# Relative-bias lines in 16 DRAM copies in place of 128, each bias tile read by eight transfers of 16 partitions

## The chip, the cores and the metric

The kernel runs on one core of a Trainium2 chip. The metric is the device time of one execution in microseconds (us); several executions are timed and the median is taken. TensorE (PE) does the matrix products, VectorE (DVE), ScalarE (ACT) and GpSimd (POOL) the elementwise work; DMA transfers are issued from the queues of SyncE (SP), POOL and ACT and carried out by 16 DMA engines.

## What is computed

Two transformer blocks over 256 tokens with 1024 features, in float32. Block 1 has a differential attention and a stick-breaking attention, each followed by a mixture of many small experts (PEER). Block 2 has four layers; their mixers are dsa (16 heads, one shared key/value head, keys chosen by an index score), swa (a window of 128 keys with sinks), mla (latent attention), and dsa again, each followed by a feed-forward part. The change touches the relative bias, which dsa and swa add to their logits:

```python
def t5_bucket(rel):
    n = jnp.maximum(rel, 0)
    ...
    return jnp.where(n < max_exact, n, large)

# dsa
    rel = pos[None, :, None] - sel
    bias = jnp.moveaxis(rel_bias[t5_bucket(rel)], -1, 1)
    logits = jnp.einsum('bqhd,bqjd->bhqj', qb, kg).astype(jnp.float32) * scale + bias
    logits = jnp.where((rel >= 0)[:, None], logits, -jnp.inf)
# swa
    rel = qi - kj
    in_band = (rel >= 0) & (rel < WINDOW)
    bias = jnp.transpose(rel_bias[t5_bucket(rel)], (2, 0, 1)).reshape(B_KV_HEADS, group, WINDOW, 2 * WINDOW)
```

The bias depends on query and key by their distance alone. So one line of 383 values for each of the 16 heads holds it all, and the row of query p is the line shifted by p.

## The kernel before

**Products and weights.** Each float32 product is made of three products of float32r parts: a weight chunk (512 KB, [128, 1024]) is loaded as raw, cast to whi (mostly on ACT, L133) and the rest taken as wlo = raw - whi (DVE or POOL, L135). The class Stream (L83) does this in the order of use: the loads go to SP's queue (L105) into three raw buffers, so a chunk's load starts when the cast and the split of the chunk three places ahead have read their buffer. TensorE multiplies the parts in `mm` (L228). The projections that make feature-major tiles (ps_fm) and those that accumulate outputs (acc) both take their chunks from this stream: in_a_wo is the output projection of the differential attention, in_peer_q the query projection of the PEER behind it.

**Order.** The program is written head by head, and a scheduler sets the order in which each engine has its instructions; an engine then works strictly in that order. The scheduler has its own simulated times of transfers, and so a change of the transfers alone can move other instructions.

**The bias lines.** `bias_lines` (L1020) runs once, in `diff_attention` at step s == 5 of ten (L644). It makes the 16 lines of 383 values by one small product, adds to them a line of masks for dsa and for swa (mk_dsa, mk_swa, 16 partitions of 383 values), and writes each to a DRAM tile (line_dsa, line_swa), one copy per query, 128 in all, 3064 KB each, from POOL's queue (L1034). In the ten steps run at once, for different heads: the projections and rotations (stage_p), the logits and the softmax (stage_l), and the weighted values (stage_t) that end in `out_parts`, which puts the head's output into oT (L481, on ACT). The output projection follows (`acc_wo`), with `x` normalised behind it.

**The reads.** `load_bias` (L1078) gives a tile B [128, 16, 256]: partition p gets, for each head, 256 values of copy p of the line, starting at 127 - p. As copy p lies 16*383 elements behind copy p - 1, one access pattern with a step of 16*383 - 1 per partition reads all of it in one transfer of 2048 KB (L1081) from POOL's queue. It is called at the start of `dsa` (L1103, layers 0 and 3) and of `swa` (L1225). Right behind it on POOL's queue come small constants: in dsa cmask (L1108, the causal mask, to which the index score is added, L1142), blk (L1109, a block matrix of ones for sums over 64 features), the gains gq and gk (L1111, L1112) and gmlp; in swa blk (L1229), gq and gk (L1231, L1232), the sinks and gmlp. B itself is needed later, head by head: in dsa POOL adds the masked score to it (mb, L1183 and L1186), in swa DVE adds it to the logits (L1306, L1309). Between the index score and these the dsa layer finds the best keys in eight rounds on DVE; ps_ks is the sum of the squared keys by blk, ps_pT the transposed weights of a head.

Of the kernel before, what the change touches and what calls it, by code (L numbers as in the profile page):

```python
# [10 lines left out]
F32 = mybir.dt.float32  # L11
# [8 lines left out]
P = 128  # L20
# [15 lines left out]
# which engine splits: GpSimd takes the lower parts of these chunks, VectorE the upper parts of those  # L36
# [46 lines left out]
class Stream:  # L83
    """Weight chunks in the order of their use: loaded ahead, split into two float32r parts ahead.

    A chunk's parts take a slot of the base pool, or of the pool that a phase lends (for its own chunks)."""
# [55 lines left out]
    def queue_behind(self, ins, n=4):  # L142
        """the next splits stand behind this instruction of the vector engine"""
        self.behind, self.n_behind = ins and ins.ins, n
# [5 lines left out]
    def lend(self, pool, bufs, names):  # L150
        """slots of a phase's pool, for the chunks from here on that bear its names"""
        self.pools.append([pool, bufs, []])
        c = self.pos
        while c < len(self.plan) and self.plan[c][0] in names:
            c += 1
        self.lent_until = c
# [5 lines left out]
    def get(self, *keys, ahead=2):  # L162
        """the parts of the next chunks, which keys name; all chunks before them are used up"""
        c = self.pos
        for k, key in enumerate(keys):
            assert self.plan[c + k] == key, (self.plan[c + k], key)
        for pool in self.pools:
            pool[2] = [d for d in pool[2] if d >= c]
        self._fill(c + len(keys) - 1 + ahead)
        assert self.split >= c + len(keys), (keys, self.split)  # L170
        self.pos += len(keys)
        return [self.done.pop(c + k) for k in range(len(keys))]
# [3 lines left out]
def tile_two_blocks(ctx: ExitStack, tc: tile.TileContext, t: dict, out: bass.AP, dbg=None):  # L176
# [40 lines left out]
    def log_exp_table(after=None):  # L217
        """the set that holds both Ln and Exp, from here on"""
# [17 lines left out]
    class Parts:  # L236
        """feature-major activations [1024, 256] in two float32r parts, by feature chunk d and token tile"""
# [16 lines left out]
    def to_hT(src, tt, hT, make=None):  # L254
        """src [128 tokens, 1024] -> feature-major parts, columns of token tile tt; make(half) fills half of src"""
# [18 lines left out]
    def proj_fm(hT, *key, M=P):  # L274
        """feature-major projection of one chunk: PSUM [M, 256]"""
# [14 lines left out]
    def proj_fm_first(hT, keys, outs):  # L290
        """the first chunks of a phase, a token tile at a time, into outs, SBUF [M, 256] each"""
# [22 lines left out]
    def acc_rows(chunks, accs, first, ahead=2, chain=None, keep=4, stop=False):  # L314
        """accs[tt][half] [128 tokens, 512] += lhs^T (128 rows) @ chunk [128, 1024], for (key, lhs(tt, part)) in chunks

        With a chain, these are the last chunks: chain(tt) follows for each token tile, the first one's beside the
        products of the second, of which the last (keep steps) wait for its transposes to have been issued."""
# [3 lines left out]
        tail = 2 if chain else 0  # of these chunks the first half of the columns comes first  # L322
# [26 lines left out]
    def acc_wo(key, oT, chain, ahead=3):  # L349
        """the output projection, a token tile at a time; chain(tt, acc) follows"""  # L350
# [7 lines left out]
    def lend(px, bufs, *names):  # L358
        """more slots for the weights of this phase"""
# [12 lines left out]
    def add_residual(tt, acc, hf, alpha=None, scale=None):  # L372
        """a half of x: x * alpha + acc, or x + acc * scale"""
# [7 lines left out]
    def rsqrt_small(dst, src, eps, scale):  # L381
        """dst = 1 / sqrt(src * scale + eps)"""
# [3 lines left out]
    def norm_residual(tt, acc, gbc, bbc, sp):  # L386
        """x = layer norm of x * alpha + acc, up to its last step, which comes back: last(half)"""
# [16 lines left out]
    def rms_to_hT(tt, gbc, hT, sp):  # L404
# [4 lines left out]
        for hf in range(2):  # h takes the squares first  # L409
# [9 lines left out]
    def gained_to_hT(tt, gbc, hT, sp, spare):  # L419
        """x * gain -> hT; the square of the rms factor, which a squared relu lets through, comes back  # L420

        spare: two PSUM banks that nothing needs any more"""
# [16 lines left out]
    def bcast(pool, src, n, tag, queue=nc.gpsimd):  # L439
        """a [n] row of DRAM on all partitions"""  # L440
# [8 lines left out]
    # ---------------------------------------------------------------- attention pieces  # L449
    def transposes_pair(p_sb, sp):  # L450
        """p_sb [128 q, 2, 384] -> SBUF [128 k, 2, 384]: (k0,q0) (k0,q1) (k1,q1)"""
# [8 lines left out]
    def av(o, pTs, h, tt, v):  # L460
        """o [128 q, dv] = p @ v for one head and query tile"""
# [6 lines left out]
    def out_parts(o_sb, g, oT, gain=None):  # L468
        """o_sb [128 t, 2 (tile), 128 features] -> feature-major parts of group g"""
# [17 lines left out]
    def softmax_sums(L, sp, src=None):  # L487
        """L [128 q, 2, 128 + width] (tile 0 | tile 1): p unnormalised, of src or in place; sums [128, tile, 2]"""
# [13 lines left out]
    def softmax_pair(L, sp):  # L502
        """p unnormalised in place, reciprocals of the sums"""
# [5 lines left out]
    def logits_pair(q_of, k_of):  # L509
        """PSUM [128 q, 2 heads, 384]: tile 0 on keys 0..127, tile 1 on keys 0..255"""  # L510
# [7 lines left out]
    def pv_group(g, p_sb, ri, v, oT, sp):  # L518
        """p @ v of a pair of 64-wide heads, normalised, transposed into oT"""
# [13 lines left out]
    # ---------------------------------------------------------------- block 1, layer 0: differential attention  # L533
    def diff_attention(hT):
        with ExitStack() as px:
# [10 lines left out]
            # the constants come behind the first weights  # L546
# [53 lines left out]
            def stage_l(g):  # L600
                qr, kr = stt.pop(g)
                ps = logits_pair(lambda h: qr[h * 64 : h * 64 + 64, :], lambda h: kr[h * 64 : h * 64 + 64, :])
                # the first 64 queries of a tile do not see the last 64 keys of its range
# [53 lines left out]
    # ---------------------------------------------------------------- block 1, layer 1: stick-breaking attention  # L657
# [74 lines left out]
    # ---------------------------------------------------------------- PEER  # L732
    def peer(layer, hT, last):
        J1 = 72  # H of the columns from here on waits in DRAM while the gates take their place
# [4 lines left out]
        with ExitStack() as px:  # L739
# [120 lines left out]
            def gate():  # L860
                """G[:, j, t] = sum over the selections of token t of the gate at (i, j): into X, or times what X holds"""
# [134 lines left out]
            for b in range(NB - 1):  # L996
                nxt = split_s(b + 1)
                if b == NA - 1:
                    # what Xa held is used up: x comes back, and more slots for the weights
# [19 lines left out]
    # ---------------------------------------------------------------- block 2  # L1019
    def bias_lines():  # L1020
        """one line per head of the relative bias, in DRAM, a copy per query: entry m is for rel = 255 - m"""
        with tc.tile_pool(name="bl", bufs=1, side="right") as bl:
# [6 lines left out]
            for nm in ("dsa", "swa"):  # L1029
# [3 lines left out]
                ln = dpool.tile([P, 16, 383], F32, name=f"line_{nm}")  # L1033
                nc.gpsimd.dma_start(ln.rearrange("p h m -> h p m"), mk.unsqueeze(1).to_broadcast([16, P, 383]))  # L1034
# [6 lines left out]
    def rope_tables():  # L1041
        """cosines and sines of the latent attention's rope, and both times the gain of q's rope features"""
        with tc.tile_pool(name="bl", bufs=1, side="right") as bl:
# [5 lines left out]
            # angles: position * frequency, reduced to [-pi, pi]  # L1049
# [11 lines left out]
            # cos first: sin(ang + pi/2); the multiple of 2 pi is taken before the quarter turn is added  # L1061
# [16 lines left out]
    def load_bias(pool, line):  # L1078
        B = pool.tile([P, 16, S], F32, name="B")
        la = line[:, :, :]  # L1080
        nc.gpsimd.dma_start(B, bass.AP(la.tensor, la.offset + 127, [[16 * 383 - 1, P], [383, 16], [1, S]]))  # L1081
# [16 lines left out]
    def dsa(a, layer, hT):  # L1098
        with ExitStack() as px:
# [49 lines left out]
            # k: normalised over its 64 features, on both halves of the partitions  # L1149
# [201 lines left out]
    def mla(layer, hT):  # L1351
        with ExitStack() as px:
# [14 lines left out]
            # latents, token-major  # L1367
# [34 lines left out]
            def rope(dst, src, tt, nh):  # L1402
                """dst, src [128, nh, 32]: rotation of the halves of 16 by the token's angles"""
# [179 lines left out]
    # ---------------------------------------------------------------- the two blocks  # L1583
# [22 lines left out]
def _fm(w, cols):  # L1606
    """[1024, *] columns -> [128, 8 * len(cols)]: feature-major chunk"""
# [130 lines left out]
```

## Time and profile before

| | |
|---|---|
| median of 3 runs | 3167.72 us (3162.14 to 3167.91) |
| span of the profiled execution | 3171.6 us |
| TensorE busy | 3045.5 us (96%) |
| VectorE busy | 2083.6 us (66%) |
| ScalarE busy | 1666.1 us (53%) |
| GpSimd busy | 316.6 us (10%) |
| moved by DMA | 551 MB, 174 GB/s |

The profile is one execution, so its span is a few microseconds from the median. A busy share is a mean over stages with different limits: an engine at 53% of the whole can still be what others wait for in one stage. The rows on which the prediction rests are in a section of their own below. In them, a line of a timeline has the start, the duration, the engine, the line of the kernel, the operation, output and inputs, and in brackets how long the engine had been idle and for what it waited; a line of DMA issues has the size of one transfer and the time from issue to landing.

### The profile page before, as it was taken

The numbers are of one execution on the slowest core, as the hardware profiler recorded it, in microseconds if no ns is written. First come the engines' busy times: TensorE is split into PE (matmuls) and PEld (weight loads), VectorE is DVE, ScalarE is ACT, GpSimd is POOL, SyncE is SP. The second block draws the span as 40 slices with busy tenths as digits, with TensorE's granted clock in tenths as the row PEclk, the third lists the DMA queues.
The fourth block names the chain that finished last, engine by engine and source line by source line (L and its number), as shares of the span: only waits on it lengthen the run. The fifth ranks groups of instructions, "written<-read, shape, count | busy, mean of one in ns | idle before, by whom it ended". The sixth has DMA issues, their size and how long they took to land.

```text
span 3171.6 us, 51266 instructions
## 1 busy us (share of the span) xinstructions
PE 3045.5 (96%) x19968; PEld 2749.4 (87%) x19968; DVE 2083.6 (66%) x3603; ACT 1666.1 (53%) x2844; POOL 316.6 (10%) x246
## 2 busy tenths in 40 slices
PE   8699999999999899999999999999999979999999
PEld 7599999978887789999988887889889968998898
DVE  5379867775555769957766555755566565556654
ACT  5434568744443634558845444554545555554553
POOL 1400000010001310000010002400120021003200
PEclk9899999999999999999999999999999999999999
DMA  6855554476655435554476654445526532654364
GB/s 202 134 161 184 174 183 165 167 264 205 225 187 179 141 125 176 177 183 167 166 252 218 231 189 155 151 160 186 184 76 216 188 108 81 194 187 148 121 201 137
DMA packets 157636, 551.05 MB, mean 174 GB/s; under 512 B 18880, under 2 KB 19712, under 8 KB 157392
## 3 DMA queue, kind: packets, MB, share of 16 engines
q1 hardware_dynamic: 135216, 489.42, 46.3%
q0 software_dynamic: 12112, 41.54, 5.4%
q10 hardware_dynamic: 10064, 16.81, 1.5%
q8 instruction: 157, 2.57, 0.3%
q14 instruction: 87, 0.71, 0.1%
HBM read 523.59 MB, written 24.10 MB: 173 GB/s over the span
## 4 chain that ended last, share of the span: by engine, by line
PE 79%; DMA 9%; DVE 6%; ACT 3%; issue 2%; POOL 1%; SPq 0%; DVEq 0%; ACTq 0%; POOLq 0%
PE acc L228 31%; PE ps_h L228 23%; PE ps_fm L228 16%; PE ps_g L228 4%; DMA hb<-h_dram 3%; ACT whi L133 1%; DVE wlo L135 1%; PE ps_av L228 1%; POOL wlo L135 1%; PE ps_l L228 1%; DMA raw<-in_a_wo_dram 1%; DMA raw<-in_dsa_in_dram 1%; DMA raw<-in_b_kq_dram 1%; DMA raw<-in_peer_q_dram 1%; PE ps_xT L262 1%
## 5 line engine op out<-in xcount | busy, mean ns | idle before, releaser
L133 ACT CAST whi<-raw 128x1024 fp32r<-128x1024 f32 (+1 forms) x908 | 947.9, 1046 | 1014.3 <-PE acc L228 273.3
L135 DVE TENSOR_TENSOR wlo<-raw,whi 128x1024 fp32r<-128x1024 f32 (+1 forms) x854 | 1043.3, 1225 | 622.7 <-ACT whi L133 621.1
L228 PE MATMUL ps_h<-hT,whi 128*128 128x256 f32 x4096 | 751.5, 284 | 0.0
L228 PE MATMUL ps_fm<-hT,whi 128*128 128x256 f32 x3424 | 664.6, 286 | 17.3 <-ACT kq L686 5.4
L228 PEld LDWEIGHTS ps_h<-hT,whi 128*128 128x128 f32 x4096 | 639.1, 191 | 1.0
L228 PEld LDWEIGHTS ps_fm<-hT,whi 128*128 128x128 f32 x3424 | 559.3, 192 | 36.6 <-DVE hT L234 6.0
L228 PE MATMUL ps_h<-hT,wlo 128*128 128x256 f32 x2048 | 584.0, 285 | 0.0
L228 PE MATMUL acc<-whi,S_parts 128*128 128x512 f32 x1984 | 537.7, 392 | 0.0
L228 PE MATMUL ps_fm<-hT,wlo 128*128 128x256 f32 (+1 forms) x1936 | 533.0, 285 | 0.0
L228 PEld LDWEIGHTS acc<-whi,S_parts 128*128 128x128 f32 x1984 | 372.8, 188 | 83.8
L228 PEld LDWEIGHTS ps_h<-hT,wlo 128*128 128x128 f32 x2048 | 391.8, 191 | 0.2
L228 PEld LDWEIGHTS ps_fm<-hT,wlo 128*128 128x128 f32 (+1 forms) x1936 | 369.7, 191 | 1.4 <-issue 0.5
L228 PE MATMUL acc<-wlo,S_parts 128*128 128x512 f32 x992 | 309.5, 393 | 5.6 <-DVE wlo L135 5.5
L135 POOL TENSOR_TENSOR wlo<-raw,whi 128x1024 fp32r<-128x1024 f32 (+1 forms) x78 | 196.1, 2525 | 1057.2 <-ACT whi L133 986.3
L228 PEld LDWEIGHTS acc<-wlo,S_parts 128*128 128x128 f32 x992 | 185.9, 188 | 49.1 <-DVE wlo L135 7.8
L228 PE MATMUL acc<-whi,hh 128*128 128x512 f32 x512 | 162.6, 393 | 0.0
L228 PE MATMUL acc<-whi,hl 128*128 128x512 f32 x512 | 161.1, 392 | 0.6 <-DVE hl L234 0.6
L228 PE MATMUL acc<-wlo,hh 128*128 128x512 f32 x512 | 161.3, 391 | 0.0
L891 DVE TENSOR_SCALAR AB<-iota,selT 128x128 f32<-128x128 f32 x512 | 142.0, 343 | 17.2 <-PE ps_g L228 17.1
L895 ACT ACTIVATE AB<-iota,selT 128x128 f32<-128x128 f32 x384 | 122.9, 392 | 36.6 <-PE ps_g L228 35.9
L228 PE MATMUL acc<-whi,oT 128*128 128x512 f32 x384 | 129.0, 420 | 12.4 <-ACT oT L481 9.7
L228 PE MATMUL ps_g<-AB 128*128 128x128 f32 x1024 | 133.8, 275 | 0.0
(353 smaller groups left out, 3207.8 us busy)
## 6 DMA issues: line engine op xcount, KB each, us to landing
raw<-in_peer_u_dram SPq DMA_DIRECT2D x256, 512.0 KB, 3.6
raw<-in_peer_v_dram SPq DMA_DIRECT2D x256, 512.0 KB, 4.3
raw<-in_up_dram SPq DMA_DIRECT2D x128, 512.0 KB, 4.2
raw<-in_dn_dram SPq DMA_DIRECT2D x128, 512.0 KB, 4.3
raw<-in_dsa_in_dram SPq DMA_DIRECT2D x30, 512.0 KB, 4.0
h_dram<-hs ACTq DMA_DIRECT2D x56, 256.0 KB, 2.2
hb<-h_dram POOLq DMA_DIRECT2D x56, 256.0 KB, 4.0
raw<-in_a_qk_dram SPq DMA_DIRECT2D x16, 512.0 KB, 3.7
```

Of the source, the lines that this page charges most:

```text
L133: self.last_hi = self.nc.scalar.copy(hi[:, :n], t[:, :n])
L135: lo_eng.tensor_tensor(lo[:, :n], t[:, :n], hi[:, :n].bitcast(F32), ALU.subtract)
L228: pe["last"] = nc.tensor.matmul(o, lhsT, rhs, start=start, stop=stop)
L262: pe["tr"] = nc.tensor.transpose(ps[:, c * P : (c + 1) * P], src[:, d * P : (d + 1) * P], ident)
L891: nc.vector.tensor_scalar(A[:, i], iota, selT[:, 0, tk : tk + 1], selT[:, 2, tk : tk + 1], ALU.is_equal, ALU.mult)
L895: nc.scalar.activation(B[:, i], iota, AF.Abs, bias=selT[:, 1, tk : tk + 1], scale=-1.0)
```

## The change

The DRAM tile of a line holds 16 copies in place of 128, and the write makes 16 (383 KB in place of 3064 KB). A transfer that steps through the copies can now serve 16 partitions. So B is read by eight transfers, each of 16 partitions and 256 KB, each starting q = 0, 16, ..., 112 elements earlier in the line. Where the rest of the source differs, it is comments.

```diff
@@ -1030,8 +1030,8 @@
-                ln = dpool.tile([P, 16, 383], F32, name=f"line_{nm}")
-                nc.gpsimd.dma_start(ln.rearrange("p h m -> h p m"), mk.unsqueeze(1).to_broadcast([16, P, 383]))
+                ln = dpool.tile([16, 16, 383], F32, name=f"line_{nm}")
+                nc.gpsimd.dma_start(ln.rearrange("p h m -> h p m"), mk.unsqueeze(1).to_broadcast([16, 16, 383]))
                 lines[nm] = ln
@@ -1078,7 +1078,10 @@
     def load_bias(pool, line):
         B = pool.tile([P, 16, S], F32, name="B")
         la = line[:, :, :]
-        nc.gpsimd.dma_start(B, bass.AP(la.tensor, la.offset + 127, [[16 * 383 - 1, P], [383, 16], [1, S]]))
+
+
+        for q in range(0, P, 16):
+            nc.gpsimd.dma_start(B[q : q + 16], bass.AP(la.tensor, la.offset + 127 - q, [[16 * 383 - 1, 16], [383, 16], [1, S]]))
         return B
```

The order of the instructions moves in a few places: in the differential attention from the line writes to the output projection, in the first part of the three layers that read B, and in the mla layer. SP's order is the same as before.

ACT, in the last heads of the differential attention, from one head's L633 to the logits' exponentials (L496) of a later head; whi_1407 to whi_1431 are consecutive chunks of in_a_wo and in_peer_q, in steps of 6. Before:

```order
L633 ACTIVATE sq,so<-ps_av,ri 128x128 x2
L383 ACTIVATE so<-so,cols 128x2
L384 ACTIVATE so<-so 128x2
L639 ACTIVATE o<-ps_av,so 128x128 x2
L133 CAST whi_1407<-raw_1393 128x1024
L133 CAST whi_1413<-raw_1399 128x1024
L481 ACTIVATE oT_362<-ps_oT,subg 128x256
L625 COPY pTs<-ps_pT 128x384
L133 CAST whi_1419<-raw_1405 128x1024
L496 ACTIVATE L,sm<-ps_l,nm 128x128 x2
L496 ACTIVATE L,sm<-ps_l,nm 128x256 x2
```

After:

```order
L633 ACTIVATE sq,so<-ps_av,ri 128x128 x2
L133 CAST whi_1419<-raw_1405 128x1024
L383 ACTIVATE so<-so,cols 128x2
L133 CAST whi_1425<-raw_1411 128x1024
L384 ACTIVATE so<-so 128x2
L639 ACTIVATE o<-ps_av,so 128x128 x2
L133 CAST whi_1431<-raw_1417 128x1024
L625 COPY pTs<-ps_pT 128x384
L481 ACTIVATE oT_362<-ps_oT,subg 128x256
L496 ACTIVATE L,sm<-ps_l,nm 128x128 x2
L496 ACTIVATE L,sm<-ps_l,nm 128x256 x2
```

At the same place of the heads two later chunks are cast: the casts have moved up by two.

POOL, at the start of swa, with the two splits (wlo) ahead of the read of B. Before:

```order
L135 TENSOR_TENSOR wlo_22145<-raw_22130,whi_22144 128x1024
L135 TENSOR_TENSOR wlo_22151<-raw_22136,whi_22150 128x1024
L1081 DMA B<-line_swa 128x16x256
L1229 DMA blk<-in_k_blk_dram 128x128
L1231 DMA gq<-in_b_q_gain_dram 64x1
L1232 DMA gk<-in_b_k_gain_dram 64x1
```

After (the buffer numbers here are higher by 7):

```order
L135 TENSOR_TENSOR wlo_22152<-raw_22137,whi_22151 128x1024
L135 TENSOR_TENSOR wlo_22158<-raw_22143,whi_22157 128x1024
L1082 DMA B<-line_swa 16x16x256 x8
L1232 DMA blk<-in_k_blk_dram 128x128
L1234 DMA gq<-in_b_q_gain_dram 64x1
L1235 DMA gk<-in_b_k_gain_dram 64x1
```

One issue has become eight at the same place, and blk, gq and gk stand behind all of them.

PE, in swa, where the sums of the squared keys (ps_ks, which need blk) stand in the second projection (ps_fm). Before:

```order
L228 MATMUL ps_fm<-hT_22106,wlo_22455 128x256
L228 MATMUL ps_fm<-hT_22106,whi_22454 128x256
L228 MATMUL ps_ks<-sqk_22425,blk 128x256
L228 MATMUL ps_ks<-sqk_22436,blk 128x256
L228 MATMUL ps_fm<-hT_22106,whi_22454 128x256
L228 MATMUL ps_fm<-hT_22106,wlo_22455 128x256
L228 MATMUL ps_fm<-hT_22107,whi_22454 128x256 x2
```

After:

```order
L228 MATMUL ps_fm<-hT_22114,whi_22468 128x256 x2
L228 MATMUL ps_fm<-hT_22114,wlo_22469 128x256
L228 MATMUL ps_ks<-sqk_22439,blk 128x256
L228 MATMUL ps_ks<-sqk_22450,blk 128x256
L228 MATMUL ps_fm<-blk,sq 128x2 x4
L228 MATMUL ps_l<-kn_22438,q 128x128
L228 MATMUL ps_l<-kn_22438,q 128x256
```

The rest of that projection has moved ahead of the two products that need blk.

## Rows read from the trace of the kernel before

**Rows 1.** Page, TensorE's busy tenths in 40 equal slices of the span:

```profile
PE   8699999999999899999999999999999979999999
```

**Rows 2.** Stretch, length, busy PE, PEld, DVE, ACT, POOL; granted clock, DMA share, GB/s:

```profile
126.00:140.00 14.00, 4.21 (x12) 3.10 (x12) 0.48 (x1) 3.61 (x5) 4.69 (x2) 0.63 1.00 164
140.00:156.00 16.00, 0.99 (x3) 0.47 (x3) 3.23 (x5) 5.27 (x19) 4.69 (x3) 0.50 1.00 164
```

**Rows 3.** Chunk loads issued from SP in 98 to 172 us: who waited, landing:

```profile
  ACT whi L133: 27.9, 5
...
DMA to landing us min/median/max: 11.7/18.9/25.8
```

**Rows 4.** The same for the chunk loads of 40 to 98 us:

```profile
DMA to landing us min/median/max: 3.3/3.5/4.6
```

**Rows 5.** Timeline of ACT in the same stretch:

```profile
160.98 0.47 ACT L481 ACTIVATE oT<-ps_oT,subg 128x256 fp32r<-128x256 f32 x1 [0.47 <-PE ps_oT L472]
```

**Rows 6.** DMA issues of 98 to 172 us: count, size, us from issue to landing:

```profile
line_dsa<-mk_dsa POOLq DMA_DIRECT2D x1, 3064.0 KB, 36.8
line_swa<-mk_swa POOLq DMA_DIRECT2D x1, 3064.0 KB, 69.6
```

**Rows 7.** DMA issues of 1977 to 1992 us, start of the first dsa layer:

```profile
B<-line_dsa POOLq DMA_DIRECT2D x1, 2048.0 KB, 15.4
...
cmask<-in_k_cmask_dram POOLq DMA_DIRECT2D x1, 192.0 KB, 15.4
```

**Rows 8.** Timeline of DVE, first dsa layer:

```profile
1993.89 0.75 DVE L1142 SCALAR_TENSOR_TENSOR score<-rl,w_sb,cmask 128x128 f32<-128x128 f32 x2 [4.77 <-DMA cmask<-in_k_cmask_dram]
...
1996.53 1.22 DVE L135 TENSOR_TENSOR wlo<-raw,whi 128x1024 fp32r<-128x1024 f32 x1
```

**Rows 9.** DMA issues of 2277 to 2292 us, start of swa:

```profile
B<-line_swa POOLq DMA_DIRECT2D x1, 2048.0 KB, 12.0
...
blk<-in_k_blk_dram POOLq DMA_DIRECT2D x1, 64.0 KB, 11.3
```

**Rows 10.** Timeline of PE in swa, the products with blk and those behind:

```profile
2289.73 1.10 PE L228 MATMUL ps_ks<-sqk,blk 128*128 128x256 f32 x4 [1.51 <-DMA blk<-in_k_blk_dram]
2290.49 0.47 PE L228 MATMUL ps_fm<-hT,whi 128*128 128x256 f32 x1
...
2292.21 0.28 PE L228 MATMUL ps_fm<-hT,wlo 128*128 128x256 f32 x1
```

**Rows 11.** DMA issues of 2876 to 2892 us, start of the second dsa layer:

```profile
B<-line_dsa POOLq DMA_DIRECT2D x1, 2048.0 KB, 11.4
```

**Rows 12.** Busy time by stretch, first dsa layer (columns as in rows 2):

```profile
1977.00:1992.00 15.00, 15.00 (x132) 14.03 (x131) 7.09 (x13) 6.67 (x11) 4.94 (x8) 1.00 0.90 300
...
1995.00:2000.00 5.00, 3.46 (x18) 2.81 (x19) 5.00 (x11) 3.12 (x5) 0.00 (x0) 0.69 0.27 84
2000.00:2010.00 10.00, 7.97 (x65) 7.62 (x65) 10.00 (x42) 4.52 (x10) 0.00 (x0) 0.99 0.37 123
```

**Rows 13.** Timeline of PE, both dsa layers: first projection matmul, first transposition of weights:

```profile
1975.46 0.38 PE L228 MATMUL ps_fm<-hT,whi 128*128 128x256 f32 x1 [0.74 <-DVE hT L234]
...
2020.02 0.31 PE L455 MATMUL ps_pT<-ident,L 128*128 128x128 f32 x1
...
2877.93 0.39 PE L228 MATMUL ps_fm<-hT,whi 128*128 128x256 f32 x1 [1.64 <-DVE hT L234]
...
2920.55 0.31 PE L455 MATMUL ps_pT<-ident,L 128*128 128x128 f32 x1
```

**Rows 14.** Timeline of POOL, both dsa layers: issue of B, first work behind it:

```profile
1977.12 1.22 POOL L1081 DMA_DIRECT2D B<-line_dsa  x1 [16.90 <-issue]
...
2015.79 0.73 POOL L1183 TENSOR_TENSOR mb<-B,score 128x256 f32<-128x256 f32 x1 [33.73 <-DVE score L1163]
...
2876.83 1.19 POOL L1081 DMA_DIRECT2D B<-line_dsa  x1 [3.29 <-ACT whi L133]
```

**Rows 15.** Page, DMA issues: transfers of 256 KB:

```profile
hb<-h_dram POOLq DMA_DIRECT2D x56, 256.0 KB, 4.0
```

More of the change, by code (lines that the diff above doesn't have):

```diff
@@ L1080, in load_bias @@
         la = line[:, :, :]
-        nc.gpsimd.dma_start(B, bass.AP(la.tensor, la.offset + 127, [[16 * 383 - 1, P], [383, 16], [1, S]]))
+        for q in range(0, P, 16):
+            nc.gpsimd.dma_start(
+                B[q : q + 16], bass.AP(la.tensor, la.offset + 127 - q, [[16 * 383 - 1, 16], [383, 16], [1, S]])
+            )
         return B
```

## The prediction

> **What bounds the kernel now.** I read the slices of the span first. TensorE's row is nearly all nines; of 40 slices of 79.3 us the second is the lowest, a 6 [rows 1]. So TensorE sets the time almost everywhere, and a DMA change counts only where TensorE waits for it. I looked at two kinds of place: the stretch in which the two lines are written (inside the second slice), and the three places at which B is read.
>
> [...] Who waits? The weight chunks requested in 98 to 172 us land 18.9 us (median) after issue, up to 25.8, and ScalarE's casts wait 27.9 us for them, five times [rows 3]; in the 58 us before, the same loads landed after 3.5 [rows 4]. ScalarE works in order: behind such a cast stands the copy that makes oT, at 160.98 us, for the output projection [rows 5]. That is how a late chunk stops TensorE. What fills the queues are the two line writes, 3064 KB each, landed 36.8 and 69.6 us after issue [rows 6].
>
> At the reads of B the margin is thin. In the first dsa layer B and cmask, queued behind it, both land after 15.4 us [rows 7], and VectorE stood 4.77 us waiting for cmask [rows 8]. In swa B took 12.0 and blk behind it 11.3 [rows 9]; TensorE waited 1.51 for blk [rows 10]. In the second dsa layer B took 11.4 [rows 11].
>
> **The change part by part.**
>
> *The line writes.* Each shrinks from 3064 to 383 KB. The first moved its bytes in 36.8 us, 85 GB/s; both were through 69.6 us after the second issue, 90 GB/s at most [rows 6]. At an eighth of the bytes both take some 9 us. Issued at the start of the stretch from 98 us, they ended near 168 before and should end near 108 now. The loads behind that should then go back towards 3.5 us. The new instruction order uses that: on ScalarE, ahead of one head's copies, stand the casts of whi_1419, 1425 and 1431 where those of 1407, 1413 and 1419 stood. The gain is at most the 27.9 us of waits of ScalarE [rows 3]. TensorE's idle time is 24.8, and the 5.2 us that it worked there ran at .63 and .50 of the clock, so that the clock has some 2 us to give back; but the normal load of 3.5 us and the chain from the last head to the projection's end stay. I subtract 3 to 8 for these: a gain of 20 to 25, and up to 28 if casts and clock give all of it. I take **25**.
>
> *The reads of B.* One transfer of 2048 KB over 128 partitions becomes eight of 256 KB over 16. What they cost is not in the trace. Let T be the time from the first issue to the landing of the last. Below, T may fall to about 13, the mean of 15.4, 12.0 and 11.4 [rows 7, 9, 11], if the same bytes move as before; eight smaller pieces could also let cmask's bytes in between, but cmask and blk stand behind all eight in one queue, so I give no gain for it. Above, the nearest row of a transfer that has 16 partitions on one side is the line write: 3064 KB in 36.8 us and 6128 KB in 69.6, which is 24.6 and 23.3 us for 2048 KB, 24 taken [rows 6]. I take **T = 19**, between the two and nearer to the second: like it, each transfer has only 16 partitions, but the line write stays on the same 16 all along, while the eight go to eight different sets and neighbours may overlap.
>
> [...] The line write moved 85 to 90 GB/s [rows 6]. [...]
>
> *What a late B delays.* On POOL's queue cmask, blk and the small gains stand behind B, as before. First dsa layer: VectorE already waits for cmask, so a delay goes straight to its score chain. VectorE is busy 10.00 of 10 us in 2000 to 2010 [rows 12], and the heads need the masked score, so it reaches TensorE. The new order draws one split of 1.22 us [rows 8] ahead of the chain, which covers that much: loss T - 15.4 - 1.2. Swa: TensorE waits for blk; the new order puts the rest of the second projection, which ran from 2290.49 to 2292.49 [rows 10], ahead of it: loss T - 12.0 - 2. Second dsa layer: here B lands 10.3 us after the first projection matmul, against 17.1 in the first layer (matmuls by [rows 13], landings by [rows 7, 11], issues at 1977.12 and 2876.83 by [rows 14]), 6.8 earlier; but the first transposition of a head's weights comes 42.6 us after it against 44.6, only 2.0 earlier [rows 13]. So 4.8 us of slack: loss T - 11.4 - 4.8. Each term is zero at least. A stall also costs clock: behind the wait for cmask, in 1995 to 2000, TensorE was busy 3.46 us at a granted .69 [rows 12], work of 2.4 us at the full clock. I add 1 us for each place, 3 in all. The loss is 3T - 43.8: at T = 19 it is 2.4 + 5.0 + 2.8 + 3 = **13.2 us**.
>
> *POOL's issues.* One issue of B took 1.22 us [rows 14]; eight take 9.8 at most. POOL's next work there is the mask sum at 2015.79, for which it had waited 33.73 us [rows 14], so the issues are hidden as instructions; they delay cmask only if they outlast the transfers that they start, which the 9.8 against T does not do.
>
> *The rest* of the diff is comments. SP's order of chunk loads is unchanged.
>
> **The sum.** -25 + 13.2 = -11.8 us. The profiled execution's span is 3171.6 us and the median of the runs 3167.7; the stalls are equally there in both, so I apply the difference to the median: **3156 us**.
>
> **The rivals.**
>
> *B's reads are not slowed (T about 13 to 15).* Then the losses are nil and the gain stands alone: 3167.7 - 25 = 3143. For it: eight sets of 16 make up the same 128 partitions, and T would hold if they were served side by side. Against: the DMA engines are busy .90 at 300 GB/s already while B loads [rows 12], so that packets that take longer have little room, and the line write with its 16 partitions kept them at 1.00 for 164 GB/s [rows 2].
>
> *The eight reads run one behind the other and cost more than the writes gave.* The place is the stall on cmask, blk and score at three layers, each time anew, while the gain comes once. It decides from T = (25 + 43.8) / 3 = 22.9 us on. At the line write's rate, T = 24, the loss is 28.2 and the time 3171. If the weight chunks, which share the engines, stretch it to 27, the loss is 37.2 and the time 3180. Wholly serial, by the row of a 256 KB transfer that lands after 4.0 us [rows 15], T = 32, a loss of 52.2 and 3195. For it: the line write's rate. Against: that last row includes the latency of each transfer, which a queue of eight need not pay eight times. [...]
>
> *The drain gets no shorter (the writes were not what TensorE waited for).* TensorE's idle time would then belong to the chain from the last heads to the output projection, and only some 10 us come back: 3167.7 - 10 + 13.2 = 3171. Against it: five waits of ScalarE name the chunks [rows 3].
>
> **How the numbers follow.** Forecast, T of 16 to 22: chance 0.50, 3147 to 3165. Reads not slowed, 3143: 0.15. Reads past the break-even, 3168 to 3195: 0.28. Drain no shorter, about 3171: 0.07. The likeliest is 3156. The range: 3141 below (a gain of 27 and no loss) and 3177 above (T of 26), which leaves out some 2 in 10: the long end of the serial reads and a gain at its bound. A measurement of this kernel tells about 0.2%, 6.3 us, from no change: 3161.4 to 3174.0. Faster takes all of the second case and five sixths of the first, 0.15 + 0.42 = 0.57. Same takes the rest of the first, 0.08, half of the third's near end and most of the fourth: 0.25. Slower is what is left, 0.18.
>
> **What would show it.** Right: chunk loads of 98 to 172 us landing after 3 to 6 us, ScalarE's waits for raw below 5 us in all, TensorE idle below 6 us in the stretch from the first head's end to the output projection, the clock at 1.00 there. For the reads: the last of the eight landing 17 to 21 us after the first issue; VectorE's wait for cmask about 2.4 us longer, TensorE's for blk about 5. Wrong: all eight landed within 13 us (second case), or after more than 23 (third); chunk loads still slow around 110 to 160 us (fourth); or a late B that nobody waits for, since heads took other work first.

## The result, and the profile after the change

The changed kernel is slower: 3183.3 us (median of 5 runs, 3180.8 to 3190.0) against 3167.7, a ratio of 1.0062 with a 95% interval of 1.0047 to 1.0078. The forecast was 3156. The profiled execution has a span of 3179.0 us. It is 7.4 us above the profiled one of before, less than the medians' 15.6: single executions of the kernel before lay between 3155.5 and 3178.9 us in all its runs, so the stages are compared by the two traces and the totals by the runs.

The drain at the line writes went as forecast. The second slice of TensorE's row is now a 9 (compare [rows 1]):

```profile
PE   8999999999999899999999998999899978998999
```

The stretches of [rows 2] in the changed kernel (length, busy PE, PEld, DVE, ACT, POOL, granted clock, DMA share, GB/s):

```profile
126.00:140.00 14.00, 11.53 (x54) 8.36 (x55) 3.80 (x11) 8.52 (x31) 2.39 (x1) 1.00 0.24 77
140.00:156.00 16.00, 14.76 (x90) 12.69 (x89) 12.03 (x17) 4.17 (x8) 6.03 (x4) 1.00 0.27 96
```

TensorE is idle for 3.7 us in place of 24.8, at the full clock; the same window holds somewhat later work now, since the drain ends earlier. That end can be read from the first statistic of x that VectorE takes behind the output projection (L395), before and after:

```profile
168.87 0.21 DVE L395 BATCH_NORM_AGGREGATE ag<-bn 128x2 f32<-128x12 f32 x1
```

```profile
143.98 0.21 DVE L395 BATCH_NORM_AGGREGATE ag<-bn 128x2 f32<-128x12 f32 x1
```

So the drain is 24.9 us shorter. The line writes, and the chunk loads of the same stretch, answer to [rows 6] and [rows 3]:

```profile
line_dsa<-mk_dsa POOLq DMA_DIRECT2D x1, 383.0 KB, 6.8
line_swa<-mk_swa POOLq DMA_DIRECT2D x1, 383.0 KB, 9.8
```

```profile
  ACT whi L133: 3.1, 3
...
DMA to landing us min/median/max: 3.5/3.6/8.4
```

The loads land after 3.6 us (median) in place of 18.9, and ScalarE's waits fall from 27.9 to 3.1 us.

The loss is in the reads of B. Issues of the first dsa layer, with the time to landing: the first of the eight, the last of the eight, and cmask:

```profile
B<-line_dsa POOLq DMA_DIRECT2D x1, 256.0 KB, 4.8
...
B<-line_dsa POOLq DMA_DIRECT2D x1, 256.0 KB, 22.9
...
cmask<-in_k_cmask_dram POOLq DMA_DIRECT2D x1, 192.0 KB, 22.7
```

The last of the eight was issued 4.0 us after the first, so T, from the first issue to the last landing, is 26.9 us, where B took 15.4 [rows 7]; 26.3 and 26.8 in the other two places. The three stretches, each from the first issue to the last landing (columns as above):

```profile
1946.00:1972.90 26.90, 21.47 (x148) 19.23 (x150) 8.76 (x15) 6.21 (x10) 8.27 (x15) 0.81 1.00 160
2261.30:2287.60 26.30, 13.50 (x89) 13.16 (x87) 7.43 (x9) 3.93 (x8) 8.29 (x15) 0.74 0.99 152
2873.10:2899.90 26.80, 22.03 (x159) 19.84 (x160) 8.76 (x15) 6.49 (x12) 8.29 (x15) 0.87 0.99 164
```

The DMA engines are busy all the time and move 152 to 164 GB/s; before, they were .90 busy and moved 300 [rows 12]. What shares them lands late, the weight chunks first of all: after 12.5 us (median) in place of 7.0. The chunk loads issued while B was read in the first dsa layer, of the kernel before:

```profile
  ACT whi L133: 2.7, 2
...
DMA to landing us min/median/max: 3.7/7.0/8.4
```

and of the changed kernel:

```profile
  ACT whi L133: 14.2, 3
...
DMA to landing us min/median/max: 6.9/12.5/18.7
```

How such a late chunk reaches TensorE is seen best in swa, in the timelines of the changed kernel's ScalarE and VectorE (two rows each) and TensorE:

```profile
2278.29 1.04 ACT L133 CAST whi<-raw 128x1024 fp32r<-128x1024 f32 x1 [11.73 <-DMA raw<-in_swa_in_dram]
2279.24 0.64 ACT L1270 COPY kn<-ps_k 128x256 f32<-128x256 f32 x2
...
2279.37 1.23 DVE L135 TENSOR_TENSOR wlo<-raw,whi 128x1024 fp32r<-128x1024 f32 x1 [13.75 <-ACT whi L133]
2280.51 0.75 DVE L1271 TENSOR_TENSOR kn<-ps_k,kn 128x256 f32<-128x256 f32 x2
...
2280.98 0.80 PE L228 MATMUL ps_fm<-hT,whi 128*128 128x256 f32 x2 [12.57 <-DVE kn L1271]
```

The chunk is late; the cast waits 11.73 us for it and the split 13.75 for the cast. kn needs neither, but its copy on ScalarE stands behind the cast, and kn itself behind the split on VectorE; TensorE waits 12.57 us for kn. In the first 54 to 70 us of the three places ScalarE's casts wait 14.2, 18.3 and 16.3 us in all for chunks, where they waited 2.7, 1.2 and 2.2 before.

POOL's queue shows a second effect (timeline of POOL, first dsa layer):

```profile
1945.96 4.52 POOL L1082 DMA_DIRECT2D B<-line_dsa  x8 [14.64 <-PE ps_xT L262]
1951.00 0.58 POOL L1111 DMA_DIRECT2D cmask<-in_k_cmask_dram  x1 [0.52 <-DMA B<-line_dsa]
...
1960.37 0.53 POOL L1115 DMA_DIRECT2D gk<-in_a_k_gain_dram  x1 [3.42 <-DMA B<-line_dsa]
...
1970.03 0.55 POOL L442 DMA_DIRECT2D gmlp<-in_norm_mlp_dram  x1 [2.33 <-DMA B<-line_dsa]
```

The eight issues take 4.52 us, but each of the seven behind them waits, 0.52 to 3.42 us, until one of the eight reads has landed: gmlp, issued 4.4 us after B before the change, is issued 24.1 us after it.

To place the difference I cut the trace at VectorE's writes of h, which end a layer's input (L415) or start the feed-forward part (L427). For the first dsa layer, of the kernel before:

```profile
1972.53 1.41 DVE L415 SCALAR_TENSOR_TENSOR h<-x,rs,gm 128x512 f32<-128x512 f32 x2 [0.60 <-ACT rs L384]
...
2083.85 1.29 DVE L427 TENSOR_TENSOR h<-x,gmlp 128x512 f32<-128x512 f32 x2
```

and of the changed kernel:

```profile
1943.18 1.41 DVE L415 SCALAR_TENSOR_TENSOR h<-x,rs,gm 128x512 f32<-128x512 f32 x2 [0.60 <-ACT rs L384]
...
2067.62 1.29 DVE L427 TENSOR_TENSOR h<-x,gmlp 128x512 f32<-128x512 f32 x2
```

The layer begins 29.4 us earlier and is 13.1 us longer (124.4 against 111.3). In the same way swa with its feed-forward part is 13.0 longer and the second dsa layer 11.2; the rest differs by -0.5. So the traces give -29.4 + 37.3 - 0.5 = +7.4 us. Of the 29.4 the drain gives 24.9; the other 4.5 arise between the drain and the first dsa layer, where the change touches nothing. That part took between 1795 and 1811 us in the traces of this document, so the 4.5 lie within the spread of single executions. The drain and the three places alone give -24.9 + 37.3 = +12.4, nearer to the medians' 15.6.

### The profile page after: what moved, and what is told of

It reads as the page before. It is cut to its first block, busy times and chain, and to the rows that moved or that the text cites. A ratio compares the mean times of both kernels' runs of the same rounds, so it can differ in the third digit from the quotient of the medians.

```text
span 3179.0 us, 51274 instructions
## 1 busy us (share of the span) xinstructions
PE 3051.7 (96%) x19968; PEld 2753.3 (87%) x19968; DVE 2084.1 (66%) x3603; ACT 1665.1 (52%) x2844; POOL 324.3 (10%) x267
## 5 line engine op out<-in xcount | busy, mean ns | idle before, releaser
L228 PE MATMUL ps_fm<-hT,whi 128*128 128x256 f32 x3424 | 672.4, 289 | 27.9 <-DVE kn L1271 12.6
L891 DVE TENSOR_SCALAR AB<-iota,selT 128x128 f32<-128x128 f32 x512 | 141.7, 341 | 17.2 <-PE ps_g L228 17.1
L962 POOL DMA_DIRECT2D hb<-h_dram x56 | 30.1, 537 | 1014.7 <-ACT whi L133 909.7
```

The source lines that it names most:

```text
L228: pe["last"] = nc.tensor.matmul(o, lhsT, rhs, start=start, stop=stop)
L891: nc.vector.tensor_scalar(A[:, i], iota, selT[:, 0, tk : tk + 1], selT[:, 2, tk : tk + 1], ALU.is_equal, ALU.mult)
L962: nc.gpsimd.dma_start(hb, h_dram[(4 * b - J1) // 2 + n])
```

## The experiments

All times are medians of 4 to 10 runs; the ratio, an estimate of its own and not the quotient of the medians, is to the kernel before, run beside it on the same chip (3169.1 us beside e1 to e4, 3165.1 beside e5 to e8, 3165.9 beside e9 to e11), with its 95% interval. T and GB/s (all DMA traffic in that stretch) are those of the first dsa layer. "Excess" is by how much the three places that read B are longer than in the trace of before; "drain" is the end of the drain as above (L395), 168.9 before.

| kernel | reads of B | T, us | GB/s | excess, us | drain | time, us | ratio |
|---|---|---|---|---|---|---|---|
| changed | 8 x 16 neighbours | 26.9 | 160 | 37.3 | 144.0 | 3183.3 | 1.0062 (1.0047 to 1.0078) |
| e1, 128 copies | 8 x 16 neighbours | 27.0 | 163 | 35.2 | 168.8 | 3205.1 | 1.0118 (1.0088 to 1.0147) |
| e2 | 1 x 128 | 11.6 | 295 | 4.4 | 144.2 | 3146.2 | 0.9947 (0.9923 to 0.9972) |
| e3 | 8 x every 8th | 18.7 | 226 | 22.6 | 145.2 | 3162.3 | 0.9975 (0.9959 to 0.9991) |
| e4, all constants first | 8 x 16 neighbours | 29.1 | 186 | 35.6 | 145.2 | 3180.8 | 1.0041 (1.0023 to 1.0059) |
| e5, 32 copies | 4 x 32 neighbours | 17.2 | 219 | 14.7 | 154.7 | 3168.4 | 1.0009 (0.9996 to 1.0022) |
| e6, 32 copies | 4 x every 4th | 11.5 | 298 | -0.1 | 151.5 | 3146.9 | 0.9944 (0.9924 to 0.9965) |
| e7, 64 copies | 2 x 64 neighbours | 17.5 | 215 | 29.1 | 162.2 | 3190.3 | 1.0069 (1.0051 to 1.0087) |
| e8, 1 reversed copy | 1 x 128 | 11.8 | 293 | 1.1 | 143.0 | 3143.1 | 0.9919 (0.9899 to 0.9940) |
| e9, small constants first | 8 x 16 neighbours | 25.9 | 179 | 29.3 | 144.5 | 3177.0 | 1.0033 (1.0015 to 1.0050) |
| e10, as e8, small constants first | 1 x 128 | 14.5 | 328 | -4.7 | 144.0 | 3138.4 | 0.9909 (0.9892 to 0.9925) |
| e11, two queues | 8 x 16 neighbours | 20.5 | 159 | 33.9 | 144.6 | 3175.8 | 1.0023 (1.0006 to 1.0041) |

The drain's gain and the excess add up: in all twelve kernels their sum is within 6.1 us of the difference of the medians. With the transfers of the changed kernel the order of the instructions moved as well; what the new order alone does, no run shows.

**The two parts alone.** e1 has the eight reads and the old writes:

```diff
-                ln = dpool.tile([16, 16, 383], F32, name=f"line_{nm}")
+                ln = dpool.tile([128, 16, 383], F32, name=f"line_{nm}")
...
-                B[q : q + 16], bass.AP(la.tensor, la.offset + 127 - q, [[16 * 383 - 1, 16], [383, 16], [1, S]])
+                B[q : q + 16], bass.AP(la.tensor, la.offset + 127 + q * (16 * 383 - 1), [[16 * 383 - 1, 16], [383, 16], [1, S]])
```

> 128 copies are written as before; B is read by eight transfers of 16 partitions, each from its own 16 copies. Theory A (sixteen neighbouring partitions): such a transfer moves at the 85 to 90 GB/s of the line write and the eight follow each other, so the last lands some 27 us after the first issue as in the changed kernel, the weight chunks beside them are slow, and each of the three places loses 11 to 13 us: nothing is gained in the drain, 3167.7 + 37 = about 3205 us. Theory C (the same few DRAM lines are read eight times over, and that is what is slow): each copy is read once here, T falls to 13 to 15 us, about 3168 to 3172. Theory B (eight transfers and issues cost by their number): as A.

e2 has the new writes and one read:

```diff
-        for q in range(0, P, 16):
-            nc.gpsimd.dma_start(
-                B[q : q + 16], bass.AP(la.tensor, la.offset + 127 - q, [[16 * 383 - 1, 16], [383, 16], [1, S]])
-            )
+        nc.gpsimd.dma_start(B, bass.AP(la.tensor, la.offset + 127, [[700, P], [383, 16], [1, S]]))
```

> 16 copies are written as in the changed kernel, and B is read by one transfer of 128 partitions from within them, with a step of 700 elements per partition (it leaves out the right shift of the lines: the bias values are wrong, bytes and packets are those of before). It gives the gain of the drain alone. A and B: B lands after 11 to 16 us, no loss at the three places, 3167.7 less 22 to 29 = 3139 to 3146 us. C: the lines read over and over keep B at 20 us or more, and the time is above 3155.

Measured: e1 3205.1, e2 3146.2. The first dsa layer's stretch from the first issue to the last landing, in e1:

```profile
1971.60:1998.60 27.00, 22.94 (x159) 20.37 (x160) 8.80 (x15) 6.84 (x12) 8.32 (x15) 0.81 0.99 163
```

and in e2:

```profile
1949.00:1960.60 11.60, 11.38 (x99) 11.26 (x101) 7.07 (x14) 4.05 (x8) 4.92 (x8) 1.00 0.84 295
```

Theory C was that the same few DRAM lines, read eight times over, are what is slow. In e1 each DRAM copy is read once and T is still 27.0: theory C falls. The reads alone cost 1.18%, 37 us; the writes alone give 0.53%, 17 us (9 to 24), or 22.9 by the medians (e2's seven runs spread from 3143.5 to 3161.5 us). The sum, some 20 us, is the measured 0.62% within the intervals. So, as far as these intervals tell, the two parts add, and the change is a true gain with a larger loss on top.

**Which partitions.** Theory A was that the set of partitions of a transfer sets its rate; theory B, that the number of transfers and issues does. e3 keeps the eight transfers of 256 KB and changes only the sets:

```diff
-        for q in range(0, P, 16):
-            nc.gpsimd.dma_start(
-                B[q : q + 16], bass.AP(la.tensor, la.offset + 127 - q, [[16 * 383 - 1, 16], [383, 16], [1, S]])
-            )
+        for q in range(8):
+            nc.gpsimd.dma_start(B[q::8], bass.AP(la.tensor, la.offset + 127 - q, [[16 * 383 - 8, 16], [383, 16], [1, S]]))
```

> 16 copies, eight transfers of 16 partitions and 256 KB as in the changed kernel, but each takes every eighth partition (q, q + 8, ...) in place of 16 neighbours. A (which 16 partitions a transfer has sets its rate): the transfers run at about twice the rate or more, T falls from 27 to 14 us or so, 3142 to 3152 us. B (number of transfers and issues): T stays at 27 and the time at 3183. C: also 27 and 3183.

Measured: 3162.3 us. B is out, since number and size of the transfers are as in the changed kernel. But T went to 18.7, not 14, and the time missed theory A's 3142 to 3152 by 10 us (e3, the first dsa layer):

```profile
1953.20:1971.90 18.70, 16.54 (x138) 15.34 (x139) 8.86 (x15) 5.90 (x11) 8.29 (x15) 1.00 0.95 226
```

The next three tell the count of partitions from the sets. In e5 32 lie side by side, in e6 the same number and size of transfers take every fourth; e7 has 64 side by side.

```diff
 e5
+                ln = dpool.tile([32, 16, 383], F32, name=f"line_{nm}")
...
+        for q in range(0, P, 32):
+                B[q : q + 32], bass.AP(la.tensor, la.offset + 127 - q, [[16 * 383 - 1, 32], [383, 16], [1, S]])
 e6, with the 32 copies of e5
+        for q in range(4):
+            nc.gpsimd.dma_start(B[q::4], bass.AP(la.tensor, la.offset + 127 - q, [[16 * 383 - 4, 32], [383, 16], [1, S]]))
 e7: as e5, with 64 for 32
```

> 32 copies, and B read by four transfers of 32 neighbouring partitions (512 KB each). By the runs so far eight transfers of 16 neighbours cost 37 us over one transfer (3183 against 3146), eight of every eighth partition 16 us (3162). Theory A1 (the count of partitions of a transfer sets its rate): twice the rate of 16, about 170 GB/s, B lands after 14 us and the time is near 3150. Theory A2 (which partitions: neighbours share a way in): about as every eighth partition, the last lands after 17 to 20 us, 3158 to 3165. Theory B (each transfer costs by itself): half of eight transfers, 3164. [...]

> 32 copies and four transfers of 32 partitions and 512 KB, as in the run beside it, but each takes every fourth partition. A1 (count) and B (number of transfers): the same time as with 32 neighbours, within 3 us. A2 (which partitions): clearly faster than 32 neighbours, B landed after 12 to 16 us, 3146 to 3152. [...]

> 64 copies, and B read by two transfers of 64 neighbouring partitions (1024 KB each). The two line writes are four times those of the changed kernel, 1532 KB, some 36 us for both, and give back a part of the drain's gain, 2 to 6 us. A1 (count of partitions): as one transfer, 3148 to 3153. B (each transfer costs): one seventh of 37 us, 3150 to 3158. A2 (which partitions): as 32 neighbours or a little better, 3160 to 3168. [...]

Measured: 3168.4 us (3 above the expected 3158 to 3165), 3146.9 (as expected) and 3190.3. The same stretch of e5:

```profile
1952.40:1969.60 17.20, 13.69 (x114) 13.42 (x116) 7.55 (x14) 3.49 (x7) 6.42 (x11) 0.94 0.95 219
```

of e6:

```profile
1953.70:1965.20 11.50, 11.32 (x98) 11.32 (x99) 6.80 (x13) 3.17 (x6) 6.36 (x11) 1.00 0.88 298
```

and of e7:

```profile
1969.30:1986.80 17.50, 14.79 (x126) 14.08 (x126) 7.56 (x14) 3.90 (x8) 5.41 (x9) 1.00 0.94 215
```

e5 and e6 differ in nothing but the sets (and the order that follows), and T is 17.2 against 11.5. Sixty-four neighbours are no faster (17.5) than thirty-two. The stretches fall into three classes: 16 neighbours at 27 us and 160 GB/s; every eighth, 32 and 64 neighbours at 17 to 19 us and 215 to 226 GB/s; every fourth and all 128 at 11.5 us and 295 GB/s. Why the sets fall into these classes, no run shows. B's own rate in them, 2048 KB in T, is 78, 112 to 122 and some 180 GB/s, beside the chunk loads.

e7 missed its expected 3160 to 3168 by 22 us at least, in two ways. Its line writes of 1532 KB each are still in the way of the drain: in 98 to 172 us ScalarE waits 19.5 us for chunks, and the drain ends at 162.2, so that 18 of the 25 us are lost again, where I had put 2 to 6.

```profile
line_dsa<-mk_dsa POOLq DMA_DIRECT2D x1, 1532.0 KB, 19.3
line_swa<-mk_swa POOLq DMA_DIRECT2D x1, 1532.0 KB, 35.3
```

And its three places lose 29.1 us where e5 loses 14.7, 11.5 of the difference in swa. There TensorE stood 10.0 us before the products with blk, which had been queued behind B and landed 18.5 us after issue (the row names the sink, landed last by the profile; the products need blk):

```profile
2302.06 2.05 PE L228 MATMUL ps_ks<-sqk,blk 128*128 128x256 f32 x4 [10.03 <-DMA sink<-in_b_sinks_dram]
```

The drain's gain does not fall in proportion to the bytes: it is 24 to 25 us with 383 KB a line (six traces), 14 and 17 with 766 (e5, e6) and 7 with 1532.

**Through constants or through chunks?** The prediction's path was cmask, blk and the gains behind B. In the first dsa layer of the changed kernel VectorE waits no longer for cmask than the 4.77 us of before [rows 8]:

```profile
1973.83 0.74 DVE L1145 SCALAR_TENSOR_TENSOR score<-rl,w_sb,cmask 128x128 f32<-128x128 f32 x2 [3.67 <-DMA cmask<-in_k_cmask_dram]
```

e4 issues all the constants ahead of B; as gmlp (512 KB) then stood ahead of B too (T 29.1 in place of 26.9), e9 leaves gmlp behind it.

```diff
-            B = load_bias(k1, lines["dsa"])
             cmask = k1.tile([P, 384], F32, name="cmask")
...
+            B = load_bias(k1, lines["dsa"])
             gmlp = bcast(k1, t["norm_mlp_2"][layer], D, "gmlp")
```

> The changed kernel, with the small constants (cmask, blk, gq, gk, sinks, gmlp) issued ahead of the eight reads of B on POOL's queue. If the loss lies in constants that are queued behind B (the prediction's path: cmask, blk, gk), it goes nearly all, and the time is 3146 to 3153. If it lies in the weight chunks, which land after 15 us in place of 4 to 8 while B is read (ScalarE waits 14 to 18 us for them at each place), most of it stays: 3175 to 3183.

> The changed kernel with cmask, blk, gq, gk and the sinks issued ahead of the eight reads, but gmlp (512 KB) left behind them; with all constants ahead the time was 3181, but gmlp stood there before B too and made B later. Constants theory (the loss comes through cmask, blk and gk that land behind B): 3150 to 3158. Starved chunks theory (the weight chunks land after 12 to 15 us while B is read, ScalarE's casts wait for them, TensorE behind): T stays near 27 and the time within 6 us of the changed kernel, 3177 to 3183; ScalarE's waits for raw stay at 14 us or more at each place.

Measured: 3180.8 and 3177.0 us, both as the starved chunks would have it, although ScalarE's waits in e9 are 12.0, 13.0 and 15.3 us at the three places and not 14 or more at each. In e9 cmask landed 2.6 us after its issue and VectorE no longer waits for it, but ScalarE still waits for chunks (waits of ScalarE in e9, 1945 to 2000 us: in total, times, longest):

```profile
ACT whi L133 <- DMA raw<-in_dsa_in_dram: 12.0, 2, 10.2
```

Its excess is 29.3 us of the 37.3. So about 8 us of the loss go with the constants, nearly all of it in swa (6.4 us longer than before, against 13.0), and 29 remain without them. The chunks are by far the largest wait left, and the excess falls with T in e3, e5 and e6 as their loads recover (landing after 9.0, 11.4 and 7.2 us in the first dsa layer, median, where the changed kernel has 12.5); but no run took the wait for chunks away and left the eight reads, so that the chunks' share is read from the traces and not isolated.

Nor are the two paths a sum. In swa of the changed kernel the products with blk came only after the 12.57 us for the chunk, and blk had just landed by then, 20.2 us after its issue at 2267.71:

```profile
2289.42 1.02 PE L228 MATMUL ps_ks<-sqk,blk 128*128 128x256 f32 x4
```

```profile
blk<-in_k_blk_dram POOLq DMA_DIRECT2D x1, 64.0 KB, 20.2
```

Without the wait for the chunk TensorE would have been there 12.57 us earlier, at 2276.9, and by these two rows would have waited an estimated 11 us for blk, as it did in swa of e7. The waits lie beside each other, and whichever ends last counts.

**Two queues.** e11 issues partitions 64 to 127 on ScalarE's queue:

```diff
-            nc.gpsimd.dma_start(
+            (nc.gpsimd if q < 64 else nc.scalar).dma_start(
```

> The changed kernel with four of the eight reads (partitions 64 to 127) issued on ScalarE's queue, the other four on POOL's. If what stops transfers from overlapping is that a queue takes them one after the other, two queues have two sets of partitions filled at once, T falls from 27 to 14 to 19 us and the time to 3150 to 3165. If the 16 DMA engines themselves are held by packets that wait for 16 partitions (their share is .99 to 1.00 in these 27 us), two queues change little: T 22 to 27, 3172 to 3185.

Measured: 3175.8 us, inside the second case, but T was 20.5, between the two cases. The first dsa layer:

```profile
1947.20:1967.70 20.50, 12.68 (x108) 12.48 (x108) 5.62 (x11) 2.75 (x5) 6.06 (x11) 0.92 1.05 159
```

B lands 6 us earlier, but the total stays at 159 GB/s with the engines full, and the chunks issued meanwhile land after 17.5 us (median) in place of 12.5. The second queue did not raise the total: most of what B wins, the chunks lose, and the two dsa layers are even 2 to 3 us longer than in the changed kernel. The whole is a little faster than the changed kernel (1.0023 against 1.0062), by its trace in swa, which is 4.4 us longer than before in place of 13.0; TensorE waits there for blk:

```profile
2285.65 2.08 PE L228 MATMUL ps_ks<-sqk,blk 128*128 128x256 f32 x4 [8.12 <-DMA blk<-in_k_blk_dram]
```

**A version that beats both.** A copy is needed only because the row of query p is the line shifted back by p. Stored in reverse, the line is read with a step of one element forward per partition: one copy, one transfer, and the users read B backwards.

```diff
-                ln = dpool.tile([16, 16, 383], F32, name=f"line_{nm}")
-                nc.gpsimd.dma_start(ln.rearrange("p h m -> h p m"), mk.unsqueeze(1).to_broadcast([16, 16, 383]))
+                mr = bl.tile([16, 383], F32, name=f"mr_{nm}")
+                nc.vector.tensor_copy(mr[:, ::-1], mk)
+                ln = dpool.tile([1, 16, 383], F32, name=f"line_{nm}")
+                nc.gpsimd.dma_start(ln.rearrange("p h m -> h p m"), mr.unsqueeze(1))
...
+        nc.gpsimd.dma_start(B, bass.AP(la.tensor, la.offset, [[1, P], [383, 16], [1, S]]))
+        return B[:, :, ::-1]
```

> A version meant to beat both: one copy of each line, stored in reverse order (24 KB), so that a step of one element per partition reads B by one transfer of 128 partitions; its users read B backwards. If neither the few DRAM lines nor the backward reads cost anything: the drain's gain and no loss, 3140 to 3147 us. If 128 partitions that read the same 24 KB slow each other, B lands after 20 us or more, and the time is 3155 to 3175.

e10 adds the small constants ahead of B, as in e9:

> The reversed line with one transfer of 128 partitions (3143), and the small constants ahead of B. If VectorE's wait for cmask (4.8 us in the kernel before) and TensorE's for blk (1.5) were on the path, these go: 3136 to 3140. If the chunks set the time there too, nothing changes: 3142 to 3146.

Measured: 3143.1 and 3138.4 us, both as expected. In e8 T is 11.8 us although all 128 partitions read the same 24 KB:

```profile
1951.40:1963.20 11.80, 11.64 (x101) 11.50 (x102) 7.55 (x14) 4.00 (x8) 4.93 (x8) 1.00 0.82 293
```

The two ratios' intervals overlap, so that the constants' share of the last step is not settled by the times; in the trace of e10 the waits for cmask and blk [rows 8, 10] are gone and the three places are 4.7 us shorter than before.

## Why the prediction was wrong

- **The gain in the drain** was right in mechanism and size: 25 us forecast; 24.9 by the end of the drain in the traces, 23.7 to 24.9 in all six with lines of 383 KB; 17 (9 to 24) by e2's ratio and 23 by its median. TensorE's idle time of 24.8 us and the clocks .63 and .50, from which the forecast took its gain, are those of 126 to 156 us [rows 2]. Each sign that was named showed: chunk loads at 3.6 us, ScalarE's waits 3.1, the clock at 1.00, TensorE idle 3.7.
- **The step that failed is T.** I took 19 us, between 13 and 24, on the reason that neighbouring transfers go to different sets and may overlap. T was 26.3 to 26.9, beyond both, and the landings follow each other: 4.8 us after its issue for the first, 22.9 for the last. 2048 KB in 26.9 us is 78 GB/s, below even the line write's 85 to 90 that I had taken for the upper bound; the total beside it, 160 GB/s, is that of the line writes' stretch, 164. e11 shows that a second queue moved B's part of this total (T 20.5) and not the total (159 GB/s). The row that held the answer was the DMA share of 1.00 at 164 GB/s beside the line write [rows 2]. I cited it, but as evidence against one rival only.
- **The path of the loss** was only half seen. I charged T through cmask, blk and the gains. The formula 3T - 43.8 gives 36.2 at 26.67, the mean of the three T, and 37.3 was found, but that agreement is luck: with the constants out of the way, e9 keeps 29.3. Nor did the signs show as named. TensorE waits for blk nowhere in the changed kernel, and VectorE's wait for cmask in the first dsa layer is shorter than before, 3.67 us against 4.77 [rows 8]; in the second it is 5.5, where there was none. In the changed kernel most goes, by the traces, through the weight chunks, which land after 12.5 us in place of 7.0 while the engines are full. I had written of the chunks only as something that could stretch T. The path through the constants is there beside it, as swa of e7 and e11 shows.
- **POOL's issues** were costed too narrowly: 9.8 us at most for eight was right (4.5), but that the issues behind them would wait for reads to land, 0.52 to 3.42 us each, was not foreseen; gmlp was issued 20 us later relative to B. No run isolates what that costs.
- **The rivals.** The one that came true is the second, at its middle price (T = 27, 3180 us), to which I gave less weight than to the overlap. T was 26.9 us with 16 neighbours, and 18.7, 17.2, 11.5 and 17.5 with the sets of e3, e5, e6 and e7; what makes a set slow, no run shows.
- **Left open.** The mla layer, which the change does not touch but whose instructions move, took 111.7 us before, 111.0 after, and 104 to 111 in the experiments; that was not traced. Nor is the share of the chunks isolated, or that of the new instruction order.

## What to carry to other kernels

A DMA that fills a few neighbouring partitions was priced here by which partitions it writes, not by its bytes alone (2048 KB in four transfers took 17.2 us into 32 neighbours each, 11.5 into every fourth), and it billed what shares the DMA engines: read the share and the GB/s together, for a share of 1.00 at 160 GB/s, where .90 had moved 300, went with chunk loads of 12.5 us in place of 7.0 in another queue. When one late thing is taken away, ask what waits beside it: of two waits that overlap, taking away the shorter gains nothing (in swa an estimated 11 of the 12.57 us would have gone to blk). If a large transfer must be cut, cut it by interleaved partitions (every fourth here, 11.5 us; every eighth still took 18.7) or, better, change the layout so that it need not be cut (e8, 11.8 us). And where the saving comes once and the price is paid at each use, count the uses first.

## What was not expected of the hardware

- The set of partitions alone, with count, size and copies the same, moved T from 17.2 us (32 neighbours) to 11.5 (every fourth), and 64 neighbours were as slow as 32 (17.5).
- Behind the eight reads on POOL's queue the next issue waited 0.52 us until one of them had landed, and each of the six after it 1.73 to 3.42: 24.1 us from B to gmlp in place of 4.4.
- Reading 24 KB of DRAM into 128 partitions of 16 KB each was no slower (11.8 us) than reading 3 MB of copies (11.4 to 15.4).
- Unchanged executions of the kernel before spread over 3155.5 to 3178.9 us, 0.7%. With 4 to 10 runs of a kernel the intervals of the ratios reach 0.13 to 0.30% to either side; the prediction had supposed 0.2%.
